# Group A's values and queries as seven products of half blocks; A's decode beside B's keys, A's attention beside B's values and queries

## The chip, the cores and the metric

The kernel runs on one core of one Trainium2 chip. The metric is the device time of one execution in microseconds (us). Before the change it is 1734.37 us, the median of three runs (1732.1 to 1738.41). One execution was profiled as well. The engines are called TensorE (PE in the profile, its weight loads PEld), VectorE (DVE), ScalarE (ACT), GpSimd (POOL) and SyncE (SP, which issues the DMAs).

## The reference, cut to what matters

One layer of a streaming encoder for a prompt of 1024 tokens and for 8 batches of 16 sample tokens with cached keys and values. All is float32. The part that matters here is the combined projection and its two head groups:

```python
h = rmsnorm(x, g_mix)                       # prompt: 1024 x 1024, sample: 128 x 1024
q_a, k_a, v_a, q_b, k_b, v_b = split_heads(h, w_in)      # each 512 columns, 8 heads of 64
# group A: stick-breaking attention
z = einsum('bqhd,bkhd->bhqk', q, k) * HEAD_DIM ** -0.5
log_keep = where(causal, log_sigmoid(-z), 0)
between = lax.cumsum(log_keep, axis=3, reverse=True) - log_keep
w = where(causal, exp(log_sigmoid(z) + between), 0)
a = einsum('bhqk,bkhd->bqhd', w, v)
# group B: softmax over the own chunk and the 8 before it, with a relative bias
```

The sample tokens attend to the cached keys and values (1024 cached rows in A, 512 in B) and to their own. New keys and values are outputs of their own, for the prompt and for the sample. After this come the output projection, a SwiGLU block, an input embedding and the final norm, in which the change touches nothing but the place of four helper functions.

## The kernel before, in words

**Number format.** A float32 matrix is held as two parts, high and low, and a product is three matmuls (`mm3`, lines 105 to 108): high by high, high by low, low by high. A split is a cast on ACT and a subtraction (`sub`, line 111) on DVE or POOL.

**Token tiles.** Tokens lie in nine tiles of 128, eight of the prompt and tile 8 of the sample. `normed` normalizes a tile, `transposed` (line 182) turns it with TensorE and splits it into `hT`, in which three tiles lie side by side.

**The projection** is the generator `qkv` (line 217). It goes through twelve pieces (`loads`, line 289), each of 256 columns of `w_in`: A's keys, A's queries, A's values, B's keys, B's values, B's queries, two pieces each. `Chunks` loads the next piece's weights (one raw buffer) and splits them (two pairs). `others` (line 248) makes keys and values: a step is one token tile, 8 x 3 matmuls of 256 columns; three steps fill a tile `st`. Keys are turned, split into a tile `sq` and stored to DRAM; values are split into `sv` and stored; both tiles share the tag "sq", with two buffers. `queries` (line 234) puts the weights on the stationary side: a step is 24 matmuls of 384 columns, and its result is already turned. One `yield` is one step, so a piece has nine steps or six.

**The order around it.** `advance(main, side, ratio, steps)` (line 725) runs `main` step by step and `ratio` steps of `side` to each. Lines 755 and 756 run 36 steps of the projection alone (A's keys and queries, then six steps of A's values). Lines 766 to 769 run 30 more, the other A values and B's keys, with R2 = 1.2 steps of A's decode to each, and then the rest of the decode; in that block TensorE takes its instructions in the order of the code. Line 778 runs the last 30 steps, B's values and queries, with 1.95 steps of A's attention to each. Elsewhere a planner that simulates a timeline sets each engine's order; all DMAs here are issued from SP's one queue.

**Decode** (`decode`, line 316) has 38 steps for A. Each loads 512 KB of cached keys and 512 KB of cached values (line 135, tile `draw`, seven buffers, six loads ahead), turns the keys on TensorE (line 389), copies them out on ACT and DVE (line 390), makes scores (412), weights (432, 433) and outputs (457). Two steps after a batch's last keys its weights are needed. Its setup reads the sample's queries, keys and values back from DRAM (349 to 358).

**Attention** (`attention`, line 504) goes through units of one head and one query tile, with a scan on DVE (583), a product on POOL (584), transposes (602) with splits (606, 111), and outputs (625, 626).

**The gate and up stage** already works with seven products of half blocks (`product`, line 1014; `first`, `sums`, `sum_parts`, and the loop from 1103).

## Time and profile before

| | |
|---|---|
| median of three runs | 1734.37 us |
| profiled execution | 1734.09 us, its span 1732.1 us |
| PE, PEld busy | 1670.1 us (96%), 1459.5 us (84%) |
| DVE, ACT, POOL busy | 1043.3 us (60%), 777.2 us (45%), 777.3 us (45%) |
| DMA | 279.93 MB, 50.0% of 16 engines' span |
| granted TensorE clock, mean | 0.995 |

The span is the time between the first and the last instruction in the profile. Matmuls are pipelined, so the mean time of one is longer than the distance from one start to the next; prices are taken from that distance. "Idle before" in a row is the time in which the engine waited just before the instruction, with the instruction that ended the wait. A line can be that of a helper: line 111 is every subtraction of a split, line 135 every raw load.

### The profile page before, as it was taken

To read this page: it belongs to the slowest core of one execution; us is meant where nothing else is said; L and a number is where in the kernel's file an instruction comes from. 1 tells how busy PE (TensorE), PEld (TensorE's weight loads), DVE (VectorE), ACT (ScalarE), POOL (GpSimd) and SP (SyncE) were. 2 spreads that over 40 slices of the span, in tenths; PEclk is the share of its full clock that TensorE was granted. 3 is DMA by queue.
4 is the path that set the end of the run, shared out by engine and by line. 5 is a ranking of instruction groups with operands and counts; after the bars stand their busy time and mean duration, and the time that the engine had idled before them with its cause. 6 is when DMAs were issued, how large, how long until landed. Compare 5 with 4: busy or idle time off the path is not lost.

```text
span 1732.1 us, 29063 instructions
## 1 busy us (share of the span) xinstructions
PE 1670.1 (96%) x11072; PEld 1459.5 (84%) x11072; DVE 1043.3 (60%) x1638; ACT 777.2 (45%) x1698; POOL 777.3 (45%) x585
## 2 busy tenths in 40 slices
PE   7999999999997999898999999999999999999998
PEld 7998888989995877787778888888888788887998
DVE  5211444257778766754886666666665698887635
ACT  5213544367767766643643333322222343333532
POOL 3213311277456412322455555555554565558364
PEclk9999999999999999999999999999999999999999
DMA  6746888666369875955422222222222774311123
GB/s 214 247 164 204 286 287 290 179 186 181 109 176 278 294 236 161 259 165 176 153 68 94 95 95 95 95 94 95 95 95 95 266 292 139 128 51 61 56 73 140
DMA packets 172715, 279.93 MB, mean 162 GB/s; under 512 B 15265, under 2 KB 103585, under 8 KB 171169
## 3 DMA queue, kind: packets, MB, share of 16 engines
q1 hardware_dynamic: 172576, 278.07, 50.0%
q8 instruction: 88, 1.44, 0.4%
q14 instruction: 51, 0.41, 0.1%
HBM read 198.47 MB, written 79.56 MB: 161 GB/s over the span
## 4 chain that ended last, share of the span: by engine, by line
PE 85%; DMA 4%; DVE 3%; ACT 3%; issue 1%; POOL 1%; SPq 1%; POOLq 0%; ACTq 0%; DVEq 0%
PE ps L1018 20%; PE ps L106 9%; PE ps L107 9%; PE ps L108 9%; PE pt L1269 6%; PE ps L1269 5%; PE pt L1018 3%; PE pt L602 2%; PE pt L389 2%; PE S L569 1%; PE po L626 1%; PE po L625 1%; PE acc L457 1%; PE S L570 1%; PE sdec L412 1%
## 5 line engine op out<-in xcount | busy, mean ns | idle before, releaser
L111 POOL TENSOR_TENSOR wlo<-wraw,whi 128x512 fp32r<-128x512 f32 (+1 forms) x128 | 226.8, 1800 | 217.6 <-ACT whi L150 217.6
L106 PE MATMUL ps<-whi,hTh 128*128 128x256 f32 x576 | 168.5, 293 | 1.7 <-ACT st L257 1.1
L107 PE MATMUL ps<-wlo,hTh 128*128 128x256 f32 x576 | 165.3, 287 | 1.0 <-POOL wlo L111 1.0
L108 PE MATMUL ps<-whi,hTl 128*128 128x256 f32 x576 | 165.5, 287 | 0.0
L150 ACT CAST whi<-wraw 128x512 fp32r<-128x512 f32 (+1 forms) x132 | 90.5, 749 | 93.5 <-PE ps L1018 66.2
L583 DVE TENSOR_TENSOR_SCAN keep<-keep,zero 128x128 f32<-128x128 f32 (+4 forms) x64 | 99.2, 1560 | 40.8 <-ACT keep L575 40.0
L106 PEld LDWEIGHTS ps<-whi,hTh 128*128 128x128 f32 x576 | 111.4, 194 | 7.9 <-issue 5.5
L584 POOL TENSOR_TENSOR w<-w,keep 128x127 f32<-128x127 f32 (+4 forms) x64 | 85.5, 1346 | 71.4 <-DVE keep L583 63.8
L107 PEld LDWEIGHTS ps<-wlo,hTh 128*128 128x128 f32 x576 | 111.3, 193 | 1.4 <-POOL wlo L111 1.3
L108 PEld LDWEIGHTS ps<-whi,hTl 128*128 128x128 f32 x576 | 111.2, 193 | 0.2 <-issue 0.2
L111 DVE TENSOR_TENSOR wtl<-pt,wth 128x512 fp32r<-128x512 f32 (+1 forms) x192 | 94.5, 514 | 17.0 <-ACT wth L606 16.5
L606 ACT CAST wth<-pt 128x512 fp32r<-128x512 f32 (+1 forms) x192 | 84.8, 464 | 39.8 <-PE pt L602 38.9
L602 PE MATMUL pt<-ident,w 128*128 128x128 f32 x528 | 87.5, 277 | 6.4 <-DVE wtl L111 2.2
L106 PE MATMUL ps<-whi,hVh 128*128 128x256 f32 x288 | 81.8, 284 | 0.5 <-ACT hVh L1416 0.5
L108 PE MATMUL ps<-whi,hVl 128*128 128x256 f32 x288 | 81.6, 284 | 0.0
L107 PE MATMUL ps<-wlo,hVh 128*128 128x256 f32 x288 | 81.4, 283 | 0.0
L569 PE MATMUL S<-qk 128*128 128x384 f32 (+2 forms) x192 | 72.4, 378 | 5.1 <-ACT keep L575 4.0
L625 PE MATMUL po<-wth,vk 128*128 128x256 f32 (+1 forms) x304 | 76.1, 282 | 1.1 <-DVE kT L390 0.9
L602 PEld LDWEIGHTS pt<-ident,w 128*128 128x128 f32 x528 | 61.8, 141 | 15.3 <-issue 5.1
L626 PE MATMUL po<-wtl,vk 128*128 128x256 f32 (+1 forms) x304 | 72.7, 282 | 0.0
L111 POOL TENSOR_TENSOR actl<-actr,acth 128x1024 fp32r<-128x1024 f32 (+1 forms) x22 | 56.7, 2577 | 33.6 <-DMA sr<-acts 18.2
L106 PE MATMUL ps<-hTh,whi 128*128 128x384 f32 x192 | 66.0, 344 | 0.0
(354 smaller groups left out, 5332.4 us busy)
## 6 DMA issues: line engine op xcount, KB each, us to landing
draw<-in_cache_sb_k SPq DMA_DIRECT2D x32, 512.0 KB, 5.2
draw<-in_cache_sb_v SPq DMA_DIRECT2D x32, 512.0 KB, 5.8
act<-sg SPq DMA_DIRECT2D x11, 1152.0 KB
actr<-act SPq DMA_DIRECT2D x22, 576.0 KB, 4.6
wraw<-in_w_in SPq DMA_DIRECT2D x12, 1024.0 KB
wraw<-in_w_gate SPq DMA_DIRECT2D x11, 1024.0 KB
wraw<-in_w_up SPq DMA_DIRECT2D x11, 1024.0 KB
v<-sv SPq DMA_DIRECT2D x36, 256.0 KB, 4.7
```

What stands on the lines that cost most here:

```text
L106: T.matmul(out, lhsT=ah, rhs=bh, start=start, stop=False)
L107: T.matmul(out, lhsT=ah, rhs=bl, start=False, stop=False)
L108: T.matmul(out, lhsT=al, rhs=bh, start=False, stop=stop)
L111: eng.tensor_tensor(out, a, hi.bitcast(F32), op=ALU.subtract)
L150: A.copy(h[:, o], v[:, o])
L569: T.matmul(sc, lhsT=hd["qq"][:, qs], rhs=hd["kkh"][:, kc], start=True, stop=False)
L583: V.tensor_tensor_scan(rev, rev, zero[:, 0:1].to_broadcast([P, n]), 1.0, op0=ALU.mult, op1=ALU.add)
L602: T.transpose(pt[:, (c - c0) * P : (c - c0 + 1) * P], w[:, c * P : (c + 1) * P], ident)
L625: T.matmul(dst, lhsT=vs, rhs=wth[:, kb - base, c0:c1], start=(i == 0), stop=False)
L626: T.matmul(dst, lhsT=vs, rhs=wtl[:, kb - base, c0:c1], start=False, stop=(i == nkb - 1))
L1018: T.matmul(out, lhsT=a[x][:, k], rhs=b[y][:, k], start=(not more and k == 0 and n == 0), stop=(k == 3 and n == 2), skip_group_check=more)
L1269: T.matmul(out, lhsT=a[i][:, x, m * P : (m + 1) * P], rhs=b[j][:, x], start=(not more and x == 0 and n == 0), stop=(x == 1 and n == 2), sk ...
```

## The change

The order of pieces becomes: A's keys, A's values, A's queries, B's keys, B's values, B's queries.

A's values and queries go through a new function, `seven`. For a piece of 256 columns the 1024 inputs, the 256 columns and the 1024 prompt tokens are halved, and the eight block products of 512 inputs by 128 columns by 512 tokens are replaced by seven products of sums of blocks (`product`, 12 matmuls of 512 columns each). The sums of the weights (`weight_sums`) are made per piece, those of the tokens (`token_sums`) once, on VectorE, beside the second half of A's keys, from unsplit copies `whole` of the transposed tokens. The sample tile stays a direct product (24 matmuls of 256). Results come with columns on the partitions; for the values each quarter is turned back (`natural`, four transposes), for the queries it is stored as it is, in splits of 256 (`quarter_out`).

`Halves` replaces `Transposed` for this stage: tokens lie four tiles side by side. `queries`, now for B alone, makes the sample tile first, like a key step with two transposes (`last_turned`), and the prompt in four steps of 24 matmuls of 512 columns. A piece of B's queries thus has five steps.

A's decode is set up after `seven`, then five steps of B's keys run alone, then 16 steps with R2 = 2.2 decode steps each (the other 13 of B's keys and three of B's values). Decode issues two loads ahead of its setup's own DMAs and the other four behind them. A's attention runs beside the other 15 steps of B's values and the 10 of B's queries, 2.3 steps to each. The first weights are loaded ahead of x. More PSUM banks serve this stage, and the pools `stg1`, `sums`, `whole` and `seven` live only there; decode's pool lies where `whole` and `seven` lay.

```diff
-R2 = 1.2
+R2 = 2.2
...
+        def spread(self, t, h, pst, whole):
...
+                A.copy(hi, p_)
+                sub(V, lo, p_, hi)
+                if t < NP:
+                    A.copy(whole[i][t // 4][:, :, s], p_)
+
+    def token_sums(whole, sums):
+
+        (p0, q0), (p1, q1) = whole
+        for j, (out, a, b) in enumerate(((p0, q0, p0), (q0, q1, q0), (q1, q1, p0), (p1, p1, q1))):
+
+            hi, lo = sums[(0, 2, 1, 3)[j]]
+            for o in (slice(0, 2), slice(2, 4)):
+                V.tensor_tensor(out[:, o], a[:, o], b[:, o], op=ALU.subtract)
+                A.copy(hi[:, o], out[:, o])
+                sub(V, lo[:, o], out[:, o], hi[:, o])
+                yield
...
+    def split_parts(stg, n, src, scale=1.0):
+        both = stg.tile([P, 2, max(n, 384)], F32R, name="sq", tag="sq")
...
+    def queries(hT, stg, grp, c, wts, bank_):
...
+        last_turned(stg, bank_, grp, 0, c, q8)
+
+        for n in range(2):
+            for pr in range(2):
+                m = slice(pr * P, (pr + 1) * P)
+                ps_ = ps["o"].tile([P, 512], F32, name="ps", tag="O")
+                for k in range(KT):
+                    mm3(ps_, wh[:, k, m], wl[:, k, m], *hT.rows(n, k), k == 0, k == KT - 1)
+                for o in (0, 256):
+                    store_parts(grp, 0, c * 2 + pr, n * 512 + o, 256,
+                                split_parts(stg, 256, ps_[:, o : o + 256], q_scale(grp, 0)))
+                yield
...
+    def seven(ch, hT, sums, stg, pp, pieces, bank, tbank, then):
+
+        (B11, _), (B21, B22) = hT.b
+        T1, T2, T3, T4 = sums
+
+        def quarter_out(piece, f, n, u):
+
+            grp, w, c = piece
+            if w < 2:
+                for o in (0, 256):
+                    store_parts(grp, w, c * 2 + f, n * 512 + o, 256, split_parts(stg, 256, u[:, o : o + 256], q_scale(grp, w)))
+
+        def natural(piece, f, n, u):
+
+            grp, w, c = piece
+            pt = tbank()
+            for t in range(4):
+                T.transpose(pt[:, t * P : (t + 1) * P], u[:, t * P : (t + 1) * P], ident)
+            st = stg.tile([P, 3, 256], F32, name="st", tag="st", bufs=2).rearrange("p a b -> p (a b)")[:, :512]
+            (V.tensor_copy if f == n else A.copy)(st, pt)
...
+            if w == 2:
+                for o in range(2):
+                    sv = stg.tile([P, 2, 384], F32R, name="sv", tag="sq").rearrange("p a b -> p (a b)")[:, :512]
...
+                    A.copy(sv[:, :, 0], pv)
+                    sub(V, sv[:, :, 1], pv, sv[:, :, 0])
...
+        def column():
+            return pp.tile([P, 512], F32, name="u", tag="u", bufs=4)
...
+        for i, piece in enumerate(pieces):
...
+            a = bank()
+            product(a, quarter(w, 0, 0), B11)
+            for x in later:
+                natural(*x)
+            later = []
+            u2 = column()
+            A.copy(u2, a)
+            e = bank()[:, :256]
+            for k in range(KT):
+                mm3(e, *hT.tok(NP, k), w[0][:, k], w[1][:, k], k == 0, k == KT - 1)
...
+            product(a, quarter(w, 1, 0), B21, True)
+            b = tbank()
+            product(b, S[1], T2)
+            c = bank()
+            product(c, S[2], T3)
+            d = bank()
+            product(d, S[0], T1)
...
+            u0 = column()
+            A.copy(u0, a)
+            quarter_out(piece, 0, 0, u0)
+            V.tensor_tensor(u2, u2, b, op=ALU.add)
+            u3 = column()
+            V.tensor_tensor(u3, u2, c, op=ALU.add)
+            product(c, quarter(w, 1, 1), T4, True)
+            V.tensor_tensor(u3, u3, d, op=ALU.add)
+            if kind < 2:
+                last_turned(stg, tbank, grp, kind, c_, e8)
+            if kind:
+                natural(piece, 0, 0, u0)
+            if more:
+                S_next = {x: weight_sum_parts(pp, x, s) for x in (1, 2, 0)}
+            product(d, S[3], B22, True)
+            quarter_out(piece, 1, 1, u3)
+            u4 = column()
+            V.tensor_tensor(u4, u2, c, op=ALU.add)
+            quarter_out(piece, 1, 0, u4)
+            V.tensor_tensor(u2, u2, d, op=ALU.add)
+            quarter_out(piece, 0, 1, u2)
+            if kind:
+                later = [(piece, 1, 1, u3), (piece, 1, 0, u4), (piece, 0, 1, u2)]
...
-        for i in range(ahead):
+        for i in range(ahead if grp else 2):
             fetch(i)
...
+        for i in range(ahead if grp else 2, ahead):
+            fetch(i)
...
-    project = qkv(ch, hT, stg)
-    advance(project, None, 0, 36)
+            hT.spread(t, normed(xp, x, g_row, t, 3), both_banks, whole)
+    project = qkv(ch, hT, stg, pieces[:2], both_banks, w_first)
+    advance(project, None, 0, 9)
+    sp = pool(s1, "sums", "right")
+    sums = [[sp.tile([P, 4, 512], F32R, name=f"T{i}{x}") for x in "hl"] for i in (1, 2, 3, 4)]
+    advance(project, token_sums(whole, sums), 1.0)
+    wstack.close()
+    pp = pool(wstack, "seven", "left")
+    w_first = seven(ch, hT, sums, stg, pp, pieces[2:6], obank, both_banks, pieces[6])
+    wstack.close()
+    s1.close()
+    stg = pool(right, "stg", "right", 2)
+    banks(first, "left", s=1)
+    project = qkv(ch, hT, stg, pieces[6:], turn_bank, w_first)
...
+    next(dec)
+    advance(project, None, 0, 5)
     with tc.manual_schedule(engines={mybir.EngineType.PE}):
-        advance(project, dec, R2, 30)
+        advance(project, dec, R2, 16)
...
-    advance(project, att, 1.95)
+    advance(project, att, 2.3)
```

More of the change, by code (lines that the diff above doesn't have):

```diff
@@ L120, in load_row @@
     def load_row(pool, src, tag):
-        t_ = pool.tile([P, D], F32, name="row_" + tag, tag=tag)
+        t_ = pool.tile([P, D], F32, name="row_" + tag, tag=tag, bufs=1)
         nc.sync.dma_start(t_, src.broadcast_to([P, D]))
@@ L180, in dst, with four @@
             return [self.t[n][g][half][:, :, o * P : (o + 1) * P] for n in range(2)]
[L182 to L192 removed]
+    def four(v):
+        return v.rearrange("p (k n) -> p k n", k=4)
```

310 lines of the change are left out of this document (190 added, 120 removed).

## The prediction

> **What bounds the kernel now.** I read the page first, then the stretches of the projection with the busy time of each engine, and then single instructions in order of time. The page:
>
> ```profile
> span 1732.1 us, 29063 instructions
> PE 1670.1 (96%) x11072; PEld 1459.5 (84%) x11072; DVE 1043.3 (60%) x1638; ACT 777.2 (45%) x1698; POOL 777.3 (45%) x585
> ```
>
> TensorE is busy 96% of the span, so what counts is the TensorE time that the change removes, and every wait of TensorE that it adds. The stretches that the change touches (columns: window and its length, busy time of PE, PEld, DVE, ACT, POOL, granted clock, DMA share, GB/s):
>
> ```profile
> 0.00:17.00 17.00, 5.48 (x22) 4.38 (x22) 8.48 (x15) 10.54 (x18) 5.33 (x14) 1.00 0.93 307
> 17.00:82.00 65.00, 64.32 (x525) 63.99 (x526) 23.81 (x41) 26.24 (x52) 17.04 (x18) 1.00 0.66 220
> 82.00:140.00 58.00, 57.93 (x359) 57.69 (x358) 8.14 (x15) 12.27 (x22) 14.61 (x7) 1.00 0.44 144
> 140.00:180.00 40.00, 37.53 (x327) 33.26 (x326) 9.59 (x12) 18.45 (x47) 14.09 (x16) 1.00 0.76 239
> 180.00:300.00 120.00, 119.65 (x1414) 105.57 (x1414) 49.80 (x74) 57.94 (x157) 22.28 (x30) 1.00 0.90 290
> 325.00:352.00 27.00, 24.12 (x217) 22.50 (x205) 7.50 (x16) 8.72 (x27) 7.13 (x9) 0.99 0.89 236
> 352.00:520.00 168.00, 167.03 (x1215) 157.78 (x1214) 126.06 (x154) 118.44 (x290) 105.42 (x78) 0.99 0.55 159
> 520.00:560.00 40.00, 29.77 (x226) 23.15 (x225) 33.10 (x48) 31.06 (x73) 27.32 (x22) 1.00 1.01 282
> ```
>
> A's keys run in 17 to 82, A's queries in 82 to 132, A's values from 132 and, with B's keys, beside the decode of A until 325; then A's attention beside B's values and queries until 520. In all of these TensorE is full; its idle time lies at the start (11.5 us), at decode's start (2.5), at attention's start (2.9) and in attention's end without cover (10.2). So a saving of TensorE time reaches the end if nothing else becomes late. In 180 to 300 DMA stands at 0.90 of its time, the nearest to a second bound.
>
> **What is removed.** Matmul prices, from start to start of instructions in order of time:
>
> ```profile
> 26.07 0.28 PE L107 MATMUL ps<-wlo,hTh 128*128 128x256 f32 x1
> ...
> 30.38 0.28 PE L107 MATMUL ps<-wlo,hTh 128*128 128x256 f32 x1
> ...
> 95.15 0.33 PE L108 MATMUL ps<-hTh,wlo 128*128 128x384 f32 x1
> ...
> 97.23 0.33 PE L108 MATMUL ps<-hTh,wlo 128*128 128x384 f32 x1
> ...
> 22.01 0.28 PE L107 MATMUL ps<-wlo,hTh 128*128 128x256 f32 x1
> 22.13 0.60 PE L189 MATMUL pt<-ident,hrow 128*128 128x128 f32 x4
> 22.49 0.37 PE L108 MATMUL ps<-whi,hTl 128*128 128x256 f32 x1
> 22.69 0.28 PE L106 MATMUL ps<-whi,hTh 128*128 128x256 f32 x1
> ```
>
> From 26.07 to 30.38 are 36 steps: 0.120 us for 256 columns. From 95.15 to 97.23 are 12: 0.173 us for 384. Four transposes between two matmuls cost 0.68 minus 0.12 for the matmul that stands in the same stretch and 0.12 for the step before it: 0.44 us, 0.11 each. The 512-column products are priced in gate and up, whose chunks already are seven products with the same code, in the chain of waits (start, length, line, count):
>
> ```profile
> 911.81 13.60 PE ps L1018 x60
> ...
> 955.95 13.60 PE ps L1018 x60
> ```
>
> 13.60/60 is 0.227 us for 512 columns; the 44.14 us between the rows are two chunks, 22.07 each, which is 84 x 0.227 + 24 x 0.120 + one transpose: in this form TensorE there waits for nothing.
>
> A half of A's values (256 columns) is now 9 x 24 x 0.120 = 25.9 us. As seven products it is 84 x 0.227 = 19.0, the sample tile 24 x 0.120 = 2.9, and 16 new transposes that bring the quarters back to token rows, 1.8: together 23.7. Saved: 2.2. A half of A's queries is now 144 x 0.173 = 24.9; it becomes 19.0 + 2.9 + two transposes 0.2 = 22.1. Saved: 2.8. Twice both: **9.9 us**. B's queries go from 144 matmuls of 384 to 96 of 512, the sample's 24 of 256 and two transposes: 21.8 + 2.9 + 0.2 = 24.9, as now: 0.
>
> **What is added, and what hides it.** *Start.* The first weights are issued ahead of x, and each token's transposed halves are copied once more on ACT.
>
> ```profile
> 3.37 0.65 SPq L135 DMA_DIRECT2D wraw<-in_w_in  x1
> ...
> 14.27 2.18 ACT L150 CAST whi<-wraw 128x512 fp32r<-128x512 f32 x4
> ...
> 17.07 0.58 PE L107 MATMUL ps<-wlo,hTh 128*128 128x256 f32 x1 [1.01 <-POOL wlo L111]
> ...
> 252.60 1.23 DVE L433 TENSOR_TENSOR wdec<-wdec,keep 128x1039 f32<-128x1039 f32 x1
> ```
>
> 1 MB ahead of x at the 307 GB/s of that stretch makes x 3.4 us later; against that the first matmuls now wait for the weights' split (the row at 17.07). Between -2 and +3.4; I take 0. The 16 copies are 16 casts of 0.55 us (a quarter of the row at 14.27), 8.7 us of ACT, which has 39 of 65 us free in 17 to 82. The token sums are eight times two DVE passes and one ACT pass over 1024 elements, 8 x 2.5 = 20 us of DVE (the row at 252.60 for one pass), beside the second half of A's keys (25.9 us); DVE has 41 us free there. Hidden, and the second key half and the first two products (another 8 us) lie ahead of the first use. Without that cover it would cost up to 20 us. The weight sums and their splits run as in gate and up, at 22.07 a chunk: 0.
>
> *The store buffers of the seven-product block.* Splits go through tag "sq", two buffers, each free only when its store has landed. Rows for one cycle, out of two groups of instructions and the landing times of the line that stores keys and queries, then ACT in order of time (idle before, and its releaser, in brackets):
>
> ```profile
> L270 ACT CAST sv<-st x36: 400/407/503, 134.2 to 417.4; 128x256 fp32r<-128x256 f32 x36
> L232 SPq DMA_DIRECT2D qT0h<-sq x12: 319/319/332, 88.2 to 133.2; - x12
> DMA to landing us min/median/max: 1.9/4.8/7.5
> ...
> 71.25 0.48 ACT L223 CAST sq<-pt 128x384 fp32r<-128x384 f32 x1
> ...
> 77.19 0.48 ACT L223 CAST sq<-pt 128x384 fp32r<-128x384 f32 x1 [1.76 <-DMA kT0l<-sq]
> ```
>
> The pass on ACT 0.41, one on DVE about the same, two issues on SP 0.64, landing 1.9 to 4.8: a cycle of 3.4 to 6.3 us, and 5.9 where it is seen (71.25 to 77.19). In the first half of A's queries 15 units want these two buffers: six left over from the values (`later`), two when the first quarter is done (8.5 us into the piece), and seven in its last 6 us. If they go without a break from 4 us on, the last one is read at 4 + 7 cycles + 0.9. It reads column u2, and the next piece needs that column by 22.1 + 5.6 = 27.7 us, in the order of the code; if the planner puts the products b, c and d first, by 35.9. A cycle of 3.4 costs 1 us, 4.0 costs 5 or 0, 5.9 costs 18.5 or 10.3. So 0 to 21. I take 3: the stores are of 128 KB instead of 192, and DMA is at 0.44 in today's query stretch, nearer to the low end. The Trainium skill, page "DMA: Bandwidth & Descriptors", section "Anatomy of one DMA — SWDGE (gpsimd) path", gives about 2.0 us plus the bytes at 436 GB/s for a DMA, so 2.3 us, an estimate, for such a store; by it the cycle is 3.8 us and the wait 4 us at most. The least landing of the rows, 1.9, agrees; their median, 4.8, does not.
>
> *Decode beside B's keys.* Its 64 loads of 512 KB now spread over 30 projection steps at 1.2 decode steps each; then over 16 at 2.2, after five steps without decode. Rows: the issue of a decode result, first and last of six of SP's queue, then the busy time of line 106 alone in 180 to 300, and the densest 6 us of DMA there; ahead of them the page's row of the key loads:
>
> ```profile
> draw<-in_cache_sb_k SPq DMA_DIRECT2D x32, 512.0 KB, 5.2
> ...
> 203.10 0.73 SPq L475 DMA_DIRECT2D mixs<-ow  x1
> ...
> 300.43 0.60 SPq L475 DMA_DIRECT2D mixs<-ow  x1
> ...
> 180.00:300.00 120.00, 48.51 (x166) 31.42 (x165) 1.00 0.90 290
> ...
> 222.00:228.00 6.00, 6.00 (x74) 5.46 (x73) 1.12 (x2) 1.99 (x5) 0.00 (x0) 1.00 1.06 382
> ```
>
> Four decode steps take 97.3/5 = 19.5 us. Line 106 ran 166 times in 120 us, so all three lines 498 x 0.120 = 59.8 us, half the time: a decode step is about (19.5 - 9.7 - 0.6 for key transposes)/4 = 2.3 us of TensorE. A round is then one projection step 2.9 + its transposes 0.2 + 2.2 x 2.3 = 8.1 us, and it moves 2.2 x 1.05 + 0.45 MB (two key stores, output, weights) = 2.76 MB: 340 GB/s, against 290 at a share of 0.90 now (322 at 1.00) and 382 in the densest stretch. The last load is issued about 14 rounds in, 114 us; to move by then are 37.6 MB (6 loads come in the five lead steps). At 290 that takes 130 us, 16 late; at 322, 117, 2.7 late; at 382 nothing. I take 2.5, by the 322. Engines keep up: DVE 50 and ACT 58 of 120 us become about 75 and 85.
>
> Decode's new region lies where the sums lay, so its loads no longer come during A's keys. Its start needs A's last query from DRAM; now that path stands in the chain of waits:
>
> ```profile
> 133.75 4.17 DMA qT0l<-sq
> 137.94 2.88 DMA sq<-qT0l
> 140.98 1.28 POOL sq L351
> ...
> 143.74 0.38 PE L106 MATMUL ps<-whi,hTh 128*128 128x256 f32 x1 [1.06 <-ACT st L257]
> ```
>
> 8.5 us (TensorE, in the last row, waits 1.1 of them, as ACT stands behind that path), against five steps of 2.9 = 14.4 us of lead: hidden unless the block's stores are 6 us behind, then up to 8.5. The same queue of SP carries it; per half piece 15 to 19 issues of 0.32 us, 6 of 22 us, so SP is not the bound.
>
> *A's attention* loses three value steps (8.6 us of TensorE) to decode and gets 25 x 2.3 = 57.5 of its steps beside the projection, not 58.5. DVE was at 126 of 168 us there, so TensorE still leads. One more unit falls into the stretch without cover (TensorE 29.8 of 40): -1 to +3, I take +1. Its first loads wait as now (325 to 352): 0.
>
> **The sum.** The profiled execution took 1734.1 us (span 1732.1 and 2.0 around it); the median shown is 1734.4. 1734.1 - 9.9 + 3 + 2.5 + 1 = 1730.7, so **1731**. A measurement of this kernel can tell about 0.5% from no change: 1725.7 and 1743.0 are the borders.
>
> **The rivals.**
> *Nothing waits.* The cycle stays below 3.3 us or the planner reorders, and DMA carries 340 GB/s. For it: gate and up wait for nothing, and 382 was reached. Against: seven splits come in the last 6 us of a query piece. Then also the wait of 1.1 us at decode's start is gone: 1734.1 - 9.9 - 1.1 = 1723.
> *Two store buffers set the pace.* Place: between the two halves of A's queries, column u2 behind "sq". It is slower than before by over 0.5% from a cycle of 5.9 us in the order of the code: 18.5 us, 1734.1 - 9.9 + 18.5 + 3.5 = 1746. For it: the row at 77.19 shows this cycle. Against: larger stores, and DMA busier there.
> *Decode becomes DMA-bound.* At today's 290 GB/s: 16 us, 1734.1 - 9.9 + 16 + 3 + 1 = 1744. For it: the share of 0.90 now; against: 290 is what was asked, not what can be had.
>
> **How the numbers follow.** The forecast with small waits 0.42 (its own range 1726 to 1743), nothing waits 0.33, store buffers 0.13, DMA-bound decode 0.10, the rest 0.02. So faster by over 0.5% 0.33, within 0.42, slower 0.25. Range: from "nothing waits" with a better start and attention, 1718, to the store buffers with a late decode start, 1750.
>
> **What would show it.** Four pieces of 22.1 to 23.7 us between A's keys and B's first key step; no wait of TensorE there behind a copy of u or a cast into sq or sv (else the second rival, with a gap near the second query half). In decode: rounds of 8.1 us, the transposes of draw not waiting for DMA, and over 320 GB/s; gaps there mean the third rival. TensorE busy time down by about 10 us. I am wrong if that sum does not fall, or if the start or A's attention moves by over 4 us.

## The result and the profile after

The changed kernel takes 1754.65 us (median of four runs, 1754.19 to 1756.53), the kernel before in the same comparison 1736.39 us (1732.1 to 1739.03): a ratio of 1.0109 with a 95% interval of 1.0095 to 1.0123. It is 18 us slower. The forecast was 1731, the range ended at 1750. The profiled execution took 1756.5 us, 22.4 more than that of before.

First the page of the kernel after, then its stretches (window and length, busy time of PE, PEld, DVE, ACT, POOL, granted clock, DMA share, GB/s):

```profile
span 1754.7 us, 28775 instructions
...
PE 1666.8 (95%) x10776; PEld 1432.4 (82%) x10776; DVE 1106.6 (63%) x1716; ACT 807.5 (46%) x1764; POOL 787.6 (45%) x593
```

```profile
0.00:20.00 20.00, 6.50 (x36) 6.50 (x36) 7.37 (x14) 11.89 (x20) 9.54 (x17) 1.00 0.91 308
20.00:86.00 66.00, 65.65 (x543) 64.70 (x542) 49.30 (x65) 43.53 (x84) 28.26 (x17) 1.00 0.44 146
86.00:175.00 89.00, 89.00 (x458) 75.77 (x456) 37.29 (x65) 35.91 (x75) 36.98 (x28) 1.00 0.57 178
175.00:200.00 25.00, 20.32 (x157) 19.08 (x157) 8.49 (x12) 6.49 (x16) 6.77 (x8) 0.93 0.83 271
200.00:220.00 20.00, 17.19 (x156) 13.62 (x155) 8.38 (x10) 9.48 (x26) 1.78 (x3) 1.00 0.95 320
220.00:337.00 117.00, 114.22 (x1464) 96.08 (x1463) 55.04 (x82) 60.79 (x167) 19.78 (x28) 0.99 0.85 289
420.00:470.00 50.00, 40.05 (x256) 34.56 (x255) 42.57 (x53) 33.33 (x86) 28.75 (x20) 0.90 0.46 121
470.00:540.00 70.00, 69.26 (x444) 59.51 (x442) 49.22 (x66) 48.04 (x116) 28.82 (x25) 1.00 0.49 140
540.00:580.00 40.00, 25.59 (x175) 21.12 (x175) 23.13 (x38) 24.05 (x57) 20.65 (x19) 0.83 0.89 270
```

TensorE is busy 3.3 us less, not 9.9, and idle 26 us more (1754.7 - 1666.8 against 1732.1 - 1670.1). The block of seven products is full (89.00 of 89). New holes stand at its end (175 to 200), in A's attention (420 to 470: 10 us idle at a clock of 0.90) and at that attention's end (540 to 580).

Busy time hides slow matmuls, so I made a ledger. Each TensorE instruction has a price, its usual distance to the next start (0.11, 0.12, 0.173 and 0.227 us for 128, 256, 384 and 512 columns, as in the prediction; the median over all runs for the rest). What an instruction takes beyond it is loss: idle time, low clock, and short instructions that follow one another more slowly than usual. The 8 us behind TensorE's last instruction are left out. Between fixed marks of the work ("qkv" is the projection):

```
loss of TensorE, us          before  after  own bank  denser decode
to 60 us (start included)     17.0    16.5    16.5      17.3
60 to 140                      0.4     0.0     0.0       0.0
140 to the end of A's decode  39.4    50.5    51.4      47.6
to the last product of qkv     8.8    23.2     8.2      11.6
to B's decode's last keys     37.4    43.9    47.3      41.4
behind that                   44.1    45.1    44.2      45.5
sum of the prices           1576.9  1566.9  1566.9    1566.9
```

The last two columns are runs told below. The prices sum to 10.0 us less: the saving is there. But 32.1 us of loss came in: 11.1 up to the end of A's decode, 14.4 while attention runs beside the projection, 6.5 from there to the last keys of B's decode and 1.0 behind them, none at the start.

The largest hole, in order of time over TensorE and then ACT (start, length, engine, line, what; idle before and its releaser):

```profile
424.07 0.39 PE L108 MATMUL ps<-hT10h,wlo 128*128 128x512 f32 x1
...
437.15 1.97 PE L803 MATMUL pt<-ident,w 128*128 128x128 f32 x8 [2.91 <-POOL w L785]
438.77 0.56 PE L826 MATMUL po<-wth,vk 128*128 128x256 f32 x1
439.13 0.41 PE L827 MATMUL po<-wtl,vk 128*128 128x256 f32 x1
439.35 0.41 PE L826 MATMUL po<-wth,vk 128*128 128x256 f32 x1
...
455.74 0.38 PE L286 MATMUL pt<-ident,q 128*128 128x128 f32 x2
...
465.30 0.50 PE L106 MATMUL ps<-hT01h,whi 128*128 128x512 f32 x1
```

```profile
404.97 0.37 ACT L298 COPY q<-ps 128x256 f32<-128x256 f32 x1
...
456.46 0.40 ACT L259 ACTIVATE sq<-pt 128x256 fp32r<-128x256 f32 x1
456.74 0.40 ACT L259 ACTIVATE sq<-ps 128x256 fp32r<-128x256 f32 x1
```

No product of the projection runs from 424.3 to 465.3. B's sample queries stand ready at 405.3 (L298), yet are turned only at 455.7 (L286): their bank comes from the tag "T" that attention's own transposes and outputs use, and so in the order of attention's steps. The splits of two finished products (L259, `sq<-ps`) stand behind theirs, so both projection banks stay full. Attention runs alone and waits for its own chain.

### The profile page after: what moved, and what is told of

Its sections match the earlier page's. It is cut to its first block, busy times and chain, and to the rows that moved or that the text cites. A ratio compares the mean times of both kernels' runs of the same rounds, so it can differ in the third digit from the quotient of the medians.

```text
span 1754.7 us, 28775 instructions
## 1 busy us (share of the span) xinstructions
PE 1666.8 (95%) x10776; PEld 1432.4 (82%) x10776; DVE 1106.6 (63%) x1716; ACT 807.5 (46%) x1764; POOL 787.6 (45%) x593
## 3 DMA queue, kind: packets, MB, share of 16 engines
q1 hardware_dynamic: 181184, 278.08, 48.9%
## 4 chain that ended last, share of the span: by engine, by line
PE 77%; DMA 10%; DVE 5%; ACT 3%; POOL 2%; issue 2%; SPq 1%; POOLq 0%; ACTq 0%; DVEq 0%
PE ps L377 22%; PE ps L106 7%; PE ps L107 7%; PE ps L108 7%; PE pt L1481 6%; PE ps L1481 4%; PE pt L377 4%; PE pt L803 2%; PE pt L590 2%; DMA v<-sv 1%; PE po L827 1%; DMA toep<-in_rel_table 1%; PE acc L658 1%; PE po L826 1%; PE S L770 1%
## 5 line engine op out<-in xcount | busy, mean ns | idle before, releaser
L111 POOL TENSOR_TENSOR wlo<-wraw,whi 128x512 fp32r<-128x512 f32 (+1 forms) x136 | 234.7, 1755 | 186.1 <-ACT whi L150 186.0
L785 POOL TENSOR_TENSOR w<-w,keep 128x127 f32<-128x127 f32 (+4 forms) x64 | 80.8, 1271 | 90.8 <-DVE keep L784 73.6
L770 PE MATMUL S<-qk 128*128 128x384 f32 (+2 forms) x192 | 72.7, 380 | 5.5 <-ACT keep L776 3.0
L111 POOL TENSOR_TENSOR S1l<-s,S1h 128x512 fp32r<-128x512 f32 x25 | 32.3, 1292 | 97.0 <-ACT S1h L404 97.0
L771 PE MATMUL S<-qk 128*128 128x384 f32 (+2 forms) x192 | 63.3, 331 | 0.4 <-DMA qk<-kT0l 0.4
L775 ACT ACTIVATE w<-S 128x512 f32<-128x512 f32 (+2 forms) x96 | 49.2, 514 | 28.5 <-PE S L773 15.8
L1481 PE MATMUL pt<-wlo,acth 128*128 128x512 f32 x160 | 62.2, 389 | 0.0
L1481 PE MATMUL pt<-whi,actl 128*128 128x512 f32 x160 | 62.2, 389 | 0.0
L826 PEld LDWEIGHTS po<-wth,vk 128*128 128x128 f32 x304 | 59.4, 195 | 3.0 <-ACT wth L807 1.7
L1486 DVE TENSOR_TENSOR x<-x,ps 128x512 f32<-128x512 f32 x70 | 46.9, 680 | 23.1 <-PE ps L108 12.7
```

Of the source, the lines that this page charges most:

```text
L111: eng.tensor_tensor(out, a, hi.bitcast(F32), op=ALU.subtract)
L770: T.matmul(sc, lhsT=hd["qq"][:, qs], rhs=hd["kkh"][:, kc], start=True, stop=False)
L826: T.matmul(dst, lhsT=vs, rhs=wth[:, kb - base, c0:c1], start=(i == 0), stop=False)
L1481: T.matmul(out, lhsT=a[i][:, x, m * P : (m + 1) * P], rhs=b[j][:, x], start=(not more and x == 0 and n == 0), stop=(x == 1 and n == 2), sk ...
```

## The experiments

Every run is compared with runs of the kernel before on the same chip; the ratio has its 95% interval. Shifts are of medians, so two runs of different comparisons are held apart to about 2 us.

### A bank of its own for the sample's queries

```diff
-        last_turned(stg, bank_, grp, 0, c, q8)
+        last_turned(stg, lambda n: ps["o"].tile([P, 512], F32, name="pt", tag="O")[:, :n], grp, 0, c, q8)
```

> Changed: in B's queries the two transposes of the sample tile write into a bank of the projection's own tag (the one that its products use, two buffers) and no longer into attention's transpose banks. All else as in the kernel after. Theory (bank coupling): the sample's queries stand ready at 405.0 us, but their transposes run at 455.7, since their bank is handed out in attention's rotation; the splits of the two finished query products stand behind them, both product banks stay full, and no product runs from 424.3 to 465.3. With a bank of its own the gap goes: TensorE's idle time between 366 and 540 falls from 11.1 us to under 4, the clock there returns to 1.00, and the time falls by 10 to 17 us. Rival (the ratio of 2.3 and the planner's early placing make the gap): the products come early all the same, the gap stays, and the time moves by under 3 us.

Measured: 1742.35 us, ratio 1.003 (1.002 to 1.004), 12.3 us below the kernel after. The transposes now follow the copy at once, and the stretch is full:

```profile
406.81 0.37 ACT L298 COPY q<-ps 128x256 f32<-128x256 f32 x1
...
407.24 0.44 PE L286 MATMUL pt<-ident,q 128*128 128x128 f32 x2
```

```profile
420.00:470.00 50.00, 50.00 (x328) 43.31 (x327) 37.25 (x52) 35.29 (x87) 22.49 (x18) 1.00 0.53 144
470.00:500.00 30.00, 30.00 (x185) 25.64 (x184) 24.34 (x31) 20.39 (x50) 16.25 (x12) 1.00 0.51 143
500.00:560.00 60.00, 46.66 (x326) 39.72 (x325) 50.10 (x63) 42.46 (x109) 36.69 (x31) 0.91 0.71 202
```

The theory holds for the gap and for the time: from 366 to 500 us TensorE idles 0.5 us, and 12.3 lies between the 10 and 17 expected. It does not hold for the whole stretch up to 540, where the idle time only falls from 11.1 to 9.8 us. The rest of the hole moved: the projection now ends at 502 instead of 534 us, and 500 to 560 lies open.

### The ratio alone

`advance(project, att, 2.3)` becomes `advance(project, att, 1.95)` in the kernel after.

> Changed: the ratio of attention steps to projection steps is 1.95 again instead of 2.3; nothing else. Theory (bank coupling): the transposes of the sample's queries are still bound to attention's banks, but 15 percent fewer attention steps stand ahead of them in the program's order, so the gap shortens by a part at most; the end of the projection moves forward against attention and leaves more attention without cover behind it. Time within 5 us of the kernel after. Rival (the ratio makes the gap): the gap from 424 to 465 goes and the time falls by over 8 us.

Measured: 1757.79 us, ratio 1.0123 (1.0108 to 1.0138). TensorE still idles 6.6 us from 420 to 450. The ratio does not make the gap. It shortens it, as expected by a part (17.1 us of loss beside the projection instead of 23.2), and the loss behind the last keys of B's decode rises from 45.1 to 51.7.

### The first weights behind the fourth token tile

The load and split of `w_first` move from ahead of the token loop to behind its tile 3.

> Changed: the first weights are loaded and split behind the fourth token tile instead of ahead of the first. Theory (the 1 MB ahead of x makes the start late): the first transposes wait until about 8.5 us instead of 13.5, A's keys end about 3 to 5 us sooner, and the time falls by 2 to 5 us. Rival (the weights are needed at once, so they only change places with x): the first products wait for the weights instead, and the time moves by under 1.5 us.

Measured: 1756.87 us, ratio 1.0122 (1.0107 to 1.0137): no gain. The first transposes start at 7.90 instead of 13.50, but the loss up to 60 us is 17.8 instead of 16.5. What starts early starts in pieces, with waits between. The late start of the kernel after costs nothing. A's keys end later than before because 14 products of the first value piece (3.2 us) already run among them.

### A third store buffer in the block

```diff
-        both = stg.tile([P, 2, max(n, 384)], F32R, name="sq", tag="sq")
+        both = stg.tile([P, 2, 384 if late else 256], F32R, name="sq", tag="sq")
...
-    stg = pool(s1, "stg1", "right", 2)
+    stg = pool(s1, "stg1", "right", 3)
```

> Changed: during A's keys and the seven products the tag sq has three buffers of 256 columns instead of two of 384 (the same space); A's keys are split and stored in a part of 256 and one of 128 columns. Theory (the store buffers are late at the end of the block): the wait of 4.3 us before 179.4 falls below 1 us, the clock of 0.87 to 0.96 after it returns to 1.00, decode starts 4 to 6 us sooner, and the time falls by 3 to 6 us. Rival (the wait is that of the last product's own chain of passes, or decode gives the gain back): the wait stays, or goes and the end moves by under 1.5 us.

The edit is shortened: with buffers of 256 columns A's keys are also stored in two parts, so there are more stores. Measured: 1760.34 us, ratio 1.0144 (1.0129 to 1.016), 5.7 above the kernel after. The wait behind column u fell to 2.25 us, not below 1, and two new ones came:

```profile
104.40 0.50 PE L382 MATMUL ps<-hT11h,S3h 128*128 128x512 f32 x1 [1.35 <-DVE u L497]
111.57 0.66 PE L430 MATMUL pt<-ident,u 128*128 128x128 f32 x4 [2.52 <-DVE u L507]
...
182.71 0.39 PE L106 MATMUL ps<-whi,hT00h 128*128 128x256 f32 x1 [2.25 <-DVE u L509]
```

From 140 us to the end of A's decode the loss fell from 50.5 to 46.1 us, but from 60 to 140, where nothing had been lost, 5.2 came in. The same edit in the stage behind, on top of the own bank, did worse:

> Changed: as the run with the own bank (1742.4 us), and beside it the stage of B's keys, values and queries has three store buffers of 256 columns instead of two of 384 (the same space; B's keys are split and stored in parts of 256 and 128). Theory (key stores wait for landings while decode's loads fill the DMA queues, and hold the transposes' bank): the waits of TensorE from 200 to 220 (2.9 us) fall below 1 us and the time falls by 2 to 4 us. Rival (one more store for each group in full queues costs as much as the third buffer gains): the time moves by under 1.5 us.

Measured: 1760.33 us, ratio 1.0135 (1.0115 to 1.0154), 18 above the run with the own bank. The loss up to the end of A's decode rose from 51.4 to 62.7; TensorE's largest new wait there is 5.6 us in eight pieces for ACT's copies of the cached keys. Of the 11.3 us of new loss 9.6 stand at the transposes of the cached keys. Why one more store for each group costs so much was not found. Since both runs add stores as well as a buffer, they do not tell whether buffers are short; they show only that this way of getting a third one does not pay.

### What holds the end of the block

One tile's instructions in 174 to 180 of the kernel after (line, engine, count: least, median and longest in ns), and the two engines beside each other:

```profile
L260 DVE SCALAR_TENSOR_TENSOR sq<-u,sq x3: 424/1447/2557, 174.8 to 179.8; 128x256 fp32r<-128x256 f32 x3
```

```profile
173.57 4.86 POOL L111 TENSOR_TENSOR wlo<-wraw,whi 128x1024 fp32r<-128x1024 f32 x2 [14.61 <-ACT whi L150]
```

```profile
179.36 0.58 PE L106 MATMUL ps<-whi,hT00h 128*128 128x256 f32 x1 [4.26 <-DVE u L504]
```

A VectorE pass of 0.42 us takes 1.45 and 2.56 us while POOL splits weights, and each ends 0.3 us behind one of POOL's two instructions. Behind both stands the sum (L504) that frees TensorE's bank. A first try cut the wrong split:

> Changed: as the run with the transposes of the sample's queries in the projection's own bank (1742.4 us), and beside it the weights of B's first key piece are split in eight parts of 256 columns instead of two of 1024. Theory (GpSimd's subtraction holds VectorE up): in the kernel after, two subtractions of 256 columns on VectorE, 0.42 us elsewhere, took 1.45 and 2.56 us from 174.8 on and ended with GpSimd's two of 2.38 and 2.52 us; behind them stands the sum whose bank TensorE waited 4.3 us for. With parts of 256 columns (0.6 us each) a VectorE pass waits 0.6 us at most, TensorE's wait at 175 to 180 falls below 2.5 us, and the time falls by 1 to 4 us. Rival (the store buffers make the wait): it stays at 4 us.

Measured: 1741.12 us, ratio 1.0027 (1.0017 to 1.0037). The split in eight parts is the one at 152.6 us; the one beside the late passes is that of B's second key piece and stayed in two. Beside the split that was cut, VectorE's passes took 0.69, 0.64 and 1.44 us instead of 1.47 and 2.61 in the run with the own bank (the 1.44 beside another subtraction of POOL); TensorE waited for none of them. The late passes still took 1.46 and 2.57 us. TensorE's wait behind them was 2.75 us, against 4.64 in the run with the own bank: part of it went though its passes got no shorter, and why is open. The right split, on top of the denser decode told below:

```diff
+            cut = (4, V) if piece == (1, 1, 0) else (2, None)
+            nxt = ch.parts(ch.raw(in_weights(pieces[i + 1]), KT, 256), KT, 256, *cut) if i + 1 < len(pieces) else None
```

and, in a second run, `(8, None)` in the place of `(4, V)`.

> Changed: as the run with the own bank, eight parts and 13 denser decode steps (1737.6 us), and beside it the low part of the weights of B's second key piece is subtracted on VectorE in four parts instead of on GpSimd in two. Theory (GpSimd's subtraction holds VectorE up): no GpSimd work runs from 172 to 178 us, the two subtractions of 256 columns that took 3.97 us together take under 1 us of VectorE's time again, TensorE's wait of 2.5 us at 178.4 falls below 1.2 us, and the time falls by 1 to 2 us. Rival (the store buffers): the wait stays within 0.5 us, since the stores before have not landed.

> Changed: as the run with the own bank, eight parts and 13 denser decode steps (1737.6 us), and beside it the split of the weights of B's second key piece is in eight parts of 256 columns instead of two of 1024. Theory (GpSimd's subtraction holds VectorE up for the length of one part): each of VectorE's two subtractions waits 0.6 us at most, together 2.2 us or less instead of 3.97, TensorE's wait of 2.5 us falls to about 1, and the time falls by 1 to 2 us. Rival: the wait stays within 0.5 us.

Measured: 1740.79 us, ratio 1.0035 (1.0023 to 1.0047), and 1739.88 us, 1.0026 (1.0014 to 1.0037). The first two rows are of the denser decode without this edit, then come three of the run on VectorE and five of the run with `(8, None)`:

```profile
173.77 3.97 DVE L260 SCALAR_TENSOR_TENSOR sq<-u,sq 128x256 fp32r<-128x256 f32 x2 [1.18 <-ACT sq L259]
...
178.39 0.38 PE L106 MATMUL ps<-whi,hT00h 128*128 128x256 f32 x1 [2.47 <-DVE u L504]
```

```profile
175.06 0.75 DVE L260 SCALAR_TENSOR_TENSOR sq<-u,sq 128x256 fp32r<-128x256 f32 x2
...
176.46 0.39 PE L106 MATMUL ps<-whi,hT00h 128*128 128x256 f32 x1 [0.69 <-DVE u L505]
182.44 0.58 PE L106 MATMUL ps<-whi,hT00h 128*128 128x256 f32 x1 [2.84 <-ACT st L323]
```

```profile
174.42 1.56 DVE L260 SCALAR_TENSOR_TENSOR sq<-u,sq 128x256 fp32r<-128x256 f32 x2 [1.75 <-ACT sq L259]
...
176.63 0.39 PE L106 MATMUL ps<-whi,hT00h 128*128 128x256 f32 x1 [0.92 <-DVE u L505]
...
190.91 1.26 POOL L551 TENSOR_TENSOR sq<-sq,sq 128x512 f32<-128x512 f32 x1 [11.99 <-DMA sq<-qT0l]
...
192.20 1.00 ACT L582 COPY qbd<-sq 64x64 f32<-64x64 f32 x4 [9.14 <-POOL sq L551]
...
194.42 0.58 PE L106 MATMUL ps<-whi,hT01h 128*128 128x256 f32 x1 [5.37 <-ACT st L323]
```

The passes went from 3.97 to 0.75 and 1.56 us, TensorE's wait from 2.47 to 0.69 and 0.92: POOL holds VectorE up, and that was this wait. The time did not fall; both runs are 2 to 3 us above the run they start from. In the run on VectorE the gain came back six microseconds later, as the store buffers at last:

```profile
181.41 0.72 ACT L259 ACTIVATE sq<-u 128x256 fp32r<-128x256 f32 x2 [6.90 <-DMA qT0l<-sq]
```

```profile
175.16 0.38 SPq L135 DMA_DIRECT2D wraw<-in_w_in  x1
175.64 1.00 SPq L265 DMA_DIRECT2D qT0l<-sq  x2
```

The raw buffer is free sooner, so the next 1 MB of weights is issued ahead of the two stores that the last query splits wait for. In the run with `(8, None)` it came back at 194.42: TensorE waits 5.37 us there, 1.50 without the edit, for ACT, which in its order stands behind the sample's queries that decode's setup reads back from DRAM.

### Attention's end: order and ratio

All on top of the own bank and the eight parts, except the first, which has only the own bank. TensorE's order written out:

```diff
-    advance(project, att, 2.3)
+    advance(project, None, 0, 6)
+    with tc.manual_schedule(engines={mybir.EngineType.PE}):
+        advance(project, att, 3.0)
```

> Changed: as the run with the own bank (1742.4 us), and beside it TensorE's order in A's attention is that of the code: six projection steps ahead, then 3.0 attention steps for each of the 19 that are left (57 instead of 57.5). Theory (the projection runs ahead and leaves attention uncovered): with the own bank the products end at about 503 us, the third pair is stored at 545 and the fourth later, and from 500 to 560 TensorE idles 13 us and has a lower clock; held to the order of the code the last product runs near the end of the fourth pair, that idle time falls to under 5 us, and the time falls by 4 to 10 us. Rival (an order that is written out waits for each latency of attention): new waits of 0.5 us or more at attention's transposes and scores all along 360 to 520, and the time stays or rises.

Measured: 1764.66 us, ratio 1.0157 (1.0132 to 1.0182). The rival holds: 35.0 us of loss beside the projection instead of 8.2, and between 345 and 620 us TensorE waits 15.3 us in twelve pieces for ACT to free the banks of the scores. Behind the projection the loss does fall, from 47.3 to 40.9, but that is less than what is paid beside it. With the eight parts as well:

> Changed: both edits of the two runs before in one kernel (weights in eight parts; TensorE's order in A's attention that of the code). If both effects hold, they add up: 5 to 14 us below the run with the own bank, at or below the kernel before (1736). If the gain at decode's start is given back in attention, no lower than the better of the two.

Measured: 1760.58 us, ratio 1.0144 (1.0118 to 1.0171): far above the first aim (1728 to 1737). The second, no lower than the better of the two (1741), is met, but the time is 19 us above it.

> Changed: as the run with the own bank and the weights in eight parts (1741.1 us), and beside it 2.55 attention steps for each projection step instead of 2.3, so that 63 of A's 64 attention steps stand ahead of the projection's end in the program. Theory (the projection ends too early for A's attention): attention moves forward against the projection, whose last product moves from about 503 to 510 us or later; the 29.7 us that TensorE loses between 500 and 600 (stalls and lower clock, start to start against the usual step of each form) fall by 4 us or more, and the time falls by 2 to 6 us. Rival (the order of the program no longer decides, since the banks do): the last product stays at 503 and the time moves by under 1.5 us.

Measured: 1746.82 us, ratio 1.007 (1.0053 to 1.0087). The last product ran at 497.1, not later (498.1 without the edit): a higher ratio does not move the projection back. The time rose by 5.7 us, which neither the theory nor the rival has; the loss from the last product to the last keys of B's decode rose from 46.7 to 51.2.

> Changed: as the run with the own bank and the weights in eight parts (1741.1 us), and beside it the ratio of the kernel before, 1.95 attention steps for each projection step, so that B's decode stands behind 49 attention steps in the program instead of 58. Theory (a gap between the projection's end and B's decode): when the last product has run, at 498 us, only 45 of A's 64 units have begun their scores (53 in the kernel before), and B's decode turns its first keys at 546.6, 48 us later (537.0 and 20 us in the kernel before); with 49 steps ahead of it B's decode starts before 530, TensorE loses 4 us or more less between 500 and 600, and the time falls by 3 to 8 us, to 1733 to 1738. Rival (B's decode waits for its own loads and setup, and TensorE's loss is attention's): it starts before 540 all the same or the loss only moves behind 550; the time moves by under 2 us.

> Changed: as the run with the own bank and the weights in eight parts (1741.1 us), and beside it 1.65 attention steps for each projection step, so that B's decode stands behind 41 attention steps, four fewer than begin beside the projection. Theory (the gap): B's decode can start as soon as its loads and setup are there, about 20 us behind the last product, no earlier than with 1.95; the time is within 3 us of that run, or higher where B's decode now takes the place of attention that B's later stages wait for. Rival (fewer steps ahead of the decode only move attention behind it): slower than the run with 2.3, above 1741.

Measured: 1745.73 us, ratio 1.0074 (1.0056 to 1.0092), and 1762.16 us, ratio 1.0159 (1.0142 to 1.0176). With 1.95, B's decode did turn its first keys at 512.7 instead of 546.6, yet the loss up to its last keys stayed (46.4 against 46.7) and that behind it rose from 43.2 to 48.9. With 1.65 both rose, to 59.6 and 52.6, as the rival has it, and the last product ran at 485.7 instead of 497.9 with 1.95. The theory of a gap between projection and B's decode fell: earlier decode only pushes attention behind it.

### How much projection attention has beside it

`R2` and the steps of `advance(project, dec, R2, ...)` are changed, and attention's ratio so that its steps stay 57 or 58 in all: first 1.7 and 21 steps (fewer left for attention), then 2.8 and 13 (more left), then 2.45 and 15 behind a lead of three steps instead of five.

> Changed: as the run with the own bank and the weights in eight parts (1741.1 us), and beside it A's decode is spread over 21 projection steps at 1.7 decode steps each instead of 16 at 2.2, so it runs beside B's keys and the first eight steps of B's values; attention has 2.9 steps for each of the 20 that are left, the same 58 in all. Theory (2.2 decode steps to one projection step are too dense): what TensorE loses in the decode stage falls from 37.6 us towards the 28.5 of the kernel before, by 4 us or more, and the time falls by as much unless attention gives it back. Rival (the loss belongs to the decode steps themselves, however they are spread): it moves by under 2 us, and the time rises or stays, since attention has 14 us less of products beside it.

> Changed: as the run with the own bank and the weights in eight parts (1741.1 us), and beside it A's decode beside 13 projection steps at 2.8 decode steps each instead of 16 at 2.2 (all within B's keys), and attention beside all 18 value steps and the 10 of the queries, 2.05 attention steps each (57 as before). Theory (the projection's products are the cover of A's attention): with three steps more beside it, more than 47 of A's 64 units have begun when the last product has run (45 now), TensorE loses 4 us or more less between 500 and 620, and the time falls by 3 to 8 us if the denser decode costs under 3 us. Rival (the loss belongs to the stage): it stays, and the time moves by under 2 us or rises by what the denser decode waits for its loads (2.8 MB in 7.2 us of TensorE: 400 GB/s).

> Changed: as the run with the own bank and the weights in eight parts (1741.1 us), and beside it three instead of five projection steps ahead of A's decode, 15 with 2.45 decode steps each, and attention beside all 18 value steps and the 10 of the queries, 2.05 attention steps each. Theory (cover of A's attention): the same gain behind 500 as in the run with 13 steps, and less price in the decode, as its steps are less dense; but the decode's setup, whose last load landed 8.8 us after its issue at 191.15, now has 8.6 us of products beside it instead of 14.4 and may cost up to 6 us. Rival: no gain behind 500.

Measured, with the run of the eight parts for comparison:

```
                    us      ratio (95%)              loss to decode's end   A's units begun at the
                                                     / beside / behind      last product (of 64)
2.2, 16, lead 5   1741.12  1.0027 (1.0017 to 1.0037)  48.6 /  6.9 / 46.7     45
1.7, 21, lead 5   1759.87  1.0137 (1.0118 to 1.0156)  47.9 / 12.3 / 61.6     32
2.8, 13, lead 5   1737.58  1.0008 (0.9996 to 1.0019)  47.6 / 11.6 / 41.4     48
2.45, 15, lead 3  1743.92  1.0048 (1.0031 to 1.0065)  51.7 / 10.4 / 41.5     48
```

"Lead" is the number of projection steps ahead of decode; "behind" goes to the last keys of B's decode. The kernel before has 53 units begun at the last product, and 37.4 us of loss behind it. Each projection step taken from attention leaves more of it uncovered, and that is where the time goes: five steps fewer cost 15 us behind the last product, three more gave 5. A's decode costs the same at 1.7, 2.2 and 2.8 steps a round, so its density is not what it pays for; a lead of three steps instead of five costs 4. The denser run pays 4.7 more beside the projection than the run of the eight parts, in these stretches:

```profile
345.00:350.00 5.00, 1.86 (x13) 1.27 (x11) 0.00 (x0) 0.94 (x5) 1.10 (x2) 1.00 1.03 300
350.00:355.00 5.00, 3.50 (x16) 3.32 (x17) 4.68 (x5) 3.99 (x12) 4.28 (x4) 0.61 0.48 169
```

DMA is full with attention's first loads while VectorE does nothing at all. This run is level with the kernel before and 1% below the kernel after; no run beat the kernel before.

## Why the prediction was wrong

- **The saving, 9.9 us: right.** The prices sum to 10.0 less. But "TensorE busy time down by about 10 us" was a poor test: it fell by 3.3, because time at a lower clock counts as busy. TensorE is busy 30.3 us at a granted clock of 0.50 in the kernel after, 13.7 before; at half speed the 16.7 us between them hold about 8 us of busy time without work.
- **The start, 0: right** (-0.5 up to 60 us), and the token sums are hidden (0.0 lost from 60 to 140).
- **The seven-product block, +3: right in size** (a wait of 4.3; 4.9 lost between 160 and 180), **wrong in mechanism**, so the size is luck. I costed the cycle of two store buffers between the two halves of A's queries; up to 175 us, well past the place where they meet, TensorE was never idle. The wait came at the very end, where POOL holds VectorE up: in the denser run, without POOL beside it, it fell from 2.47 to 0.69. That POOL made all of the 4.3 in the kernel after is not shown, since the cut of the other split took 4.64 to 2.75. The second rival named the place about right, and its cause showed only once this one was taken away. The prediction's 2.3 us for a store comes from a section on DMAs that GpSimd issues, as its title says, while SP issues these; from 86 to 200 us the line that issues them shows 1.9 us to landing in the median and 7.6 at most.
- **Decode's setup, hidden by five steps: right here** (TensorE waits 0.2 us behind ACT at 193.37), **but with little to spare.** In the run with `(8, None)` the same path cost 5.4 us. With three steps of lead the loss rose by 4, with waits of 2.6 us at 191 and 3.4 us at 312; whether the setup makes them was not tested.
- **Decode beside B's keys, +2.5: too small.** The step is the round of 8.1 us. Four decode steps, 1.82 rounds, took 62.07/4 = 15.5 us:

```profile
237.30 0.73 SPq L676 DMA_DIRECT2D mixs<-ow  x1
...
299.37 0.59 SPq L676 DMA_DIRECT2D mixs<-ow  x1
```

  That is 8.5 us a round, 0.4 x 16 = 6.8 us more; the ledger has 11.1 less some 5 for the block, so 6. The third rival did not come: DMA carried 320 GB/s from 200 to 220 us and 289 from 220 to 337, TensorE waited for no load of the cache, and the density did not matter. The ledger says where the 6 us lie: 4.4 at the transposes of the cached keys (6.2 us of loss, 1.8 before), and most of the rest in a stretch at a clock of 0.50 from 278.2 to 281.6. The longest waits of TensorE from 185 to 337 (in all, times, longest):

```profile
PE pt L590 <- DVE sq L111: 2.2, 3, 1.5
PE pt L590 <- DVE kT L591: 1.8, 2, 1.0
```

  The first is for splits of B's keys, whose transposes take their bank from the same tag as those of the cached keys. That this shared bank is the cause was not tested.
- **A's attention, +1: the step that failed** (14.4 us more beside the projection, 6.5 behind it). The prediction's own sign for it, a move of over 4 us, came; none of its rivals names it. "TensorE still leads" was read from 126 of 168 us of DVE, an average. It left out that B's sample queries had become two transposes in attention's own bank tag; I had costed these at 0.2 us of TensorE and never asked which bank they take. Price: 12.3 us. And "one more unit falls into the stretch without cover" was eight (53 begun before, 45 with the bank freed): 9.9 us more behind the projection's end in that run, 9.3 with the eight parts, of which three steps given back recovered 5.3. Why 48 units and not 53 have begun then is open.

With the bank freed and attention's steps given back, the profiled run (1740.3 us; the median is 1737.6) still loses 16.3 us more than before: 8.2 up to decode's end, 2.8 beside the projection, 4.0 behind it and 1.4 after that. So waits and low clock take back the saving of 10 us of TensorE. Each edit also makes the planner set a new order; how much of the shifts comes from that alone, no run shows.

## What to carry to other kernels

Price a new small operation by the buffer it takes as well as by its time: two transposes in a shared rotating bank tied a free-running stage to a slow one and cost 12 us. Projection work that fills another stage's waits is not idle cargo; moving it to a stage that was full already uncovers that stage. When a wait is removed, look at which transfer is issued earlier for it.

## What the runs showed of the hardware

A subtraction on VectorE whose inputs both lie in SBUF is held up while POOL subtracts from SBUF: 1.45 to 2.62 us instead of 0.42 in the four passes that began during one of POOL's subtractions of 128x1024. The same operation out of PSUM is not: nine of its 16 passes began during a product of POOL on tiles in SBUF, and none took over 0.43 us. In the kernel after (count: least, median, longest in ns):

```profile
L260 DVE SCALAR_TENSOR_TENSOR sq<-u,sq x16: 420/426/2617, 142.8 to 181.0; 128x256 fp32r<-128x256 f32 x16
L260 DVE SCALAR_TENSOR_TENSOR sq<-ps,sq x16: 398/412/426, 460.7 to 539.1; 128x256 fp32r<-128x256 f32 x16
```

The block made the queries come from an SBUF column instead of a PSUM bank, and so exposed them. The Trainium skill, page "SBUF — State Buffer", section "Who interferes with whom", states this: a VectorE instruction with two SBUF inputs contends with a GpSimd instruction that reads SBUF, and the loser waits for the whole of it. The trace agrees (1.45 and 2.56 us, each ending 0.3 us behind one of POOL's 2.38 and 2.52), and I had not used it.

Behind the wait of 2.91 us that ends at 437.15, matmuls of 256 columns start 0.22 us apart (439.13 to 439.35), half speed. The granted clock was 0.50 from 435.2 to 442.0, so it fell 1 us into that wait. In the 3.4 us ahead of the fall TensorE was busy for almost half the time; the rest was a wait of 0.84 us and the first microsecond of the long one (columns as in the stretches above):

```profile
431.80:435.20 3.40, 1.60 (x12) 1.11 (x10) 3.40 (x7) 2.39 (x6) 3.40 (x2) 1.00 0.99 227
435.20:438.60 3.40, 1.45 (x7) 1.45 (x8) 1.61 (x3) 1.26 (x3) 3.40 (x4) 0.50 0.08 16
```

The Trainium skill, page "TensorE: Matmul & The Clock Gate", section "Part 1: The HAM clock gate", gives an idle window of about 3.4 us for this. The trace differs: here the clock fell without a wait of that length. At 278.2 it fell behind waits of 0.97 and 0.82 us, the second not yet over, with TensorE busy for half of the 3.4 us before:

```profile
274.78:278.19 3.41, 1.73 (x28) 1.05 (x16) 3.41 (x4) 1.49 (x4) 0.14 (x1) 1.00 1.01 368
```
